# Down-projection tail in three token parts instead of two: one step of a hybrid decoder layer on one Trainium2 core

## The chip, the cores and the metric

The kernel runs on one core of a Trainium2 chip. The time is device microseconds from the launch of the one program to its end. The kernel before takes 2843.49 us (median of three runs, 2843.31 to 2844.28). The profiled execution, to which every row below belongs, is a fourth run of 2844.88 us; its instructions span 2842.7 us of that.

Names of engines: PE is TensorE's matmul side, PEld its weight loads, DVE the vector engine, ACT the scalar engine, POOL GpSimd, SP the engine that issues most DMAs. An AP is an access pattern, PSUM the memory that matmuls write.

## The reference

One layer of a decoder. 512 prompt tokens and 8 x 4 sample tokens, 544 columns in all, go through the same weights:

```
h = rmsnorm(x);  proj = h @ w_in          # mixer: SSD heads and a conformer convolution group
x = x + concat(y, u) @ w_out
h = rmsnorm(x);  u = causal_dwconv(h @ w_up)
g, v = split(u);  x = x + (silu(g) * v) @ w_down      # 43*128 inputs -> 2048 outputs
y = rmsnorm(x, norm_final_w)              # xf * rsqrt(mean(xf * xf) + 1e-5) * w
```

The change touches the last part of `@ w_down` and the final norm. The norm's mean goes over all 2048 outputs of a token, so no token can be scaled before every output tile of that token is finished.

## The kernel before, in words

Tokens are columns: an activation tile is 128 channels by 544 tokens, held as `[128, 2, 272]`, two halves of `NH` = 272 columns. A product in full precision is made of three passes in a rounded 4-byte type (`F32R`): every operand is split in a high and a low part, and `mms` issues weight-high times input-high, weight-high times input-low and weight-low times input-high, all into one PSUM tile. Each of these matmuls is preceded by its own load of a 128x128 weight tile, so the program has as many weight loads as matmuls.

The down-projection adds up 43 input tiles `a` (128 channels each) into 16 output tiles `xres`. Chunks of inputs are taken in turn by a list of work items. The last chunk, `ktail` = 39 with `ntail` = 4 input tiles, is held back: its activations are in `Ah` and `Al`, its weights for all 16 output tiles are loaded and split during the items before (`keep_prep`) and stay in SBUF as `keep[t]`. What is left at the very end is `last_half`: 16 output tiles, 4 inputs, 3 passes, 2 token halves.

`last_half` is written out in order, and every engine runs its instructions in that order. It goes over the halves on the outside and the 16 output tiles inside. For one tile and one half it issues

- 12 matmuls of 272 columns into an `aux` PSUM tile (`paux` has four of them),
- on DVE the sum with the residual `x` (L1512),
- on ACT the square of `x` (L1514) and a copy scaled with the norm weight into `ot`, one tile for two output tiles (L1523),
- on POOL the running sum of the squares (L1518; the last square is not added but goes to the next step by itself).

When a half is complete, `rs_half` sums the squares over the partitions with two matmuls by a matrix of ones (L1486), and DVE and ACT work out the reciprocal root (L1490 to L1497). For the first half this is laid behind the tiles t = 1 to 4 of the second, and `scale_out`, which multiplies an `ot` tile by the root (L1457) and stores it (L1458), behind the tiles after them. For the second half there is nothing left to lay it behind: `run_now(rs_half(1))` and eight `scale_out` stand one after another.

Of the kernel before, what the change touches and what calls it, by code (L numbers as in the profile page):

```python
# [10 lines left out]
AF = mybir.ActivationFunctionType  # L11
ALU = mybir.AluOpType
# [3 lines left out]
NH = 272  # L16
# [9 lines left out]
EPS = 1e-5  # L26
# [3 lines left out]
def hymba_step_kernel(ctx: ExitStack, tc: tile.TileContext, a: dict):  # L30
    nc = tc.nc
    V, G, S, T, Y = nc.vector, nc.gpsimd, nc.scalar, nc.tensor, nc.sync
# [24 lines left out]
    def nm(p):  # L57
        cnt[0] += 1
        return f"{p}{cnt[0]}"

    def slot(p, shape=None, dt=F32, side=False):
        return (Cur.side if side else slots).tile(shape or [128, 2, NH], dt, tag="s", name=nm(p))

    def aux(shape=None):
        return paux.tile(shape or [128, 512], F32, tag="a", name=nm("ax"))
# [11 lines left out]
    def flat(t):  # L77
        return t.rearrange("p h x -> p (h x)")

    def halves(ap):  # L80
        return ap.rearrange("p (h x) -> p h x", h=2)
# [106 lines left out]
    def drain_later():  # L188
        while later:
            later.popleft()()  # L190
# [29 lines left out]
    def mms(outs, hfs, h, l, nk, k0, K, rhs):  # L220
        for kk in range(nk):
            k = k0 + kk
            xh, xl = rhs(k)
            c = slice(kk * 128, kk * 128 + 128)
            passes = ((h, xh, k == 0, False), (h, xl, False, l is None and k == K - 1), (l, xh, False, k == K - 1))
            for w, x, first, last in passes[:2 if l is None else 3]:
                for o, hf in zip(outs, hfs):
                    T.matmul(o, lhsT=w[:, c], rhs=x[:, hf, :], start=first, stop=last)  # L228


    ones = const.tile([128, 128], F32, name="ones")
# [23 lines left out]
    def run_now(gen):  # L255
        for _ in gen:
            pass
# [9 lines left out]
    with tc.manual_schedule():  # L267
# [20 lines left out]
        nw = const.tile([128, 5, 16], F32, name="nw")  # L288
        Y.dma_start(out=nw, in_=a["nvec"])
        NW_MIX, NW_SSD, NW_FFN, NW_FIN, DSK = range(5)  # L290
# [800 lines left out]
        xres, xs, T_t = {}, {}, {}  # L1091
# [267 lines left out]
        Ah, Al, ar = {}, {}, {}  # L1359
# [74 lines left out]
        k0 = 0  # L1434
        for c, (n, pn) in enumerate(DOWN):
            q = len(items)
# [10 lines left out]
        ktail, ntail = k0, HID - k0  # L1447
        a_prep(range(ktail, HID), len(items) - 16)

        fin = {}  # L1450

        ot = {}

        def scale_out(i, hf):

            o = ot.pop((i, hf))
            V.tensor_tensor(o, o, fin[hf, "r"].unsqueeze(1).to_broadcast([128, 2, NH]), ALU.mult)  # L1457
            Y.dma_start(out=a["o_y"][i, hf], in_=flat(o))  # L1458

        keep = {}  # L1460

# [17 lines left out]

        keep_prep(ktail, ntail, len(items) - 16)  # L1480

        def rs_half(hf):
            p = aux()
            accs = [fin[hf], fin[hf, "last"]]
            for i, q in enumerate(accs):
                T.matmul(p[:, 0:NH], lhsT=ones, rhs=q[:, 0:NH], start=i == 0, stop=i == 1)  # L1486
            v = slot("fv")
            r, t = v[:, 1, :], slot("ft")[:, 0, :]
            v = v[:, 0, :]
            V.tensor_scalar(v, p[:, 0:NH], 1.0 / 2048.0, EPS, ALU.mult, ALU.add)  # L1490
            S.activation(r, v, AF.Sqrt)
            yield
            V.reciprocal(r, r)  # L1493
            yield
            V.tensor_tensor(t, r, r, ALU.mult)
            V.scalar_tensor_tensor(t, t, -0.5, v, ALU.mult, ALU.mult)
            V.scalar_tensor_tensor(r, t, 1.5, r, ALU.add, ALU.mult)  # L1497
            fin[hf, "r"] = r
            yield

        def last_half(k0, n):
            gen = []
            todo = deque()
            for hf in range(2):
                if hf:
                    gen.append(rs_half(0))
                for t in range(16):
                    h, l = keep[t]
                    ps = aux()
                    mms([ps[:, 0:NH]], (hf,), h, l, n, 0, n, lambda k: (Ah[k0 + k], Al[k0 + k]))  # L1510
                    x = xres[t][:, hf, :]
                    V.tensor_tensor(x, ps[:, 0:NH], x, ALU.add)  # L1512
                    sq = slot("sq", [128, NH])
                    S.activation(sq, x, AF.Square)  # L1514
                    if t == 0:
                        fin[hf] = sq
                    elif t < 15:
                        G.tensor_tensor(fin[hf], fin[hf], sq, ALU.add)  # L1518
                    else:
                        fin[hf, "last"] = sq  # L1520
                    if t % 2 == 0:
                        ot[t // 2, hf] = slot("ot")
                    S.activation(ot[t // 2, hf][:, t % 2, :], x, AF.Copy, scale=nw[:, NW_FIN, t:t + 1])  # L1523
                    if gen and t >= 1:
                        if next(gen[0], 1) == 1:
                            gen.clear()
                            todo.extend(range(8))
                    if todo:
                        scale_out(todo.popleft(), 0)
            while todo:  # L1530
                scale_out(todo.popleft(), 0)
            run_now(rs_half(1))
            for i in range(8):
                scale_out(i, 1)


        run_jobs()
# [10 lines left out]
        for i in range(3):  # L1548
            n = min(29, 86 - 29 * i)
# [20 lines left out]
            product(q)  # L1570
        evac(len(items) - 1)
        drain_later()
        last_half(ktail, ntail)
        for name in list(pools)[::-1]:
            swap(None, name)

# [107 lines left out]
```

## Time and profile before

| what | us |
|---|---|
| median of three runs | 2843.49 |
| the profiled execution | 2844.88 |
| its span, first to last instruction | 2842.7 |
| PE busy in the span | 2795.5 |
| first residual sum of `last_half` (L1512) begins | 2779.84 |
| last residual sum of `last_half` begins | 2827.62 |
| end of the span | 2842.7 |

PE is busy for 98% of the span, so the first question is what keeps it busy and the second what comes after its last matmul. In the views, times are from the start of the span; `x12` counts instructions, `[0.38 <-POOL sq L1518]` is how long the engine had been idle and what ended that. The profiled execution lies 1.4 us over the median of the runs, and 2.2 us of it lie outside the span.

### The profile page before, as it was taken

The page shows a single profiled execution, that of the slowest core. Times are in us where ns is not written, and L with a number is a line of the kernel's source. Part 1 is how long each engine was busy: PE and PEld are TensorE (multiplying, and loading weights), DVE is VectorE, ACT ScalarE, POOL GpSimd, SP SyncE. Part 2 cuts the span into 40 slices and gives each one's busy share as a digit, 9 for nine tenths or more (in the row PEclk, how much of TensorE's full clock was granted, in tenths as well). Part 3 has the DMA queues.
Part 4 walks back from the last instruction along what each step waited for, and adds up shares of the span by engine and source line. Part 5 has one row for each costly group of instructions (what it writes and reads, how often), then busy time and mean ns, then how long its engine had stood idle before and what let it go on. Part 6 is the DMA issues. An engine that isn't in the chain of part 4 may idle for free. (4 is left out here: it accounts for less than half of the span.)

```text
span 2842.7 us, 55478 instructions
## 1 busy us (share of the span) xinstructions
PE 2795.5 (98%) x22214; PEld 2755.1 (97%) x22214; DVE 2090.9 (74%) x3180; ACT 1210.9 (43%) x1792; POOL 905.5 (32%) x922
## 2 busy tenths in 40 slices
PE   7999999999999999999999999999999999999998
PEld 7999998999999999999999999999999999999997
DVE  7576565777777778335488888888888887778775
ACT  4545444333333324333344444444444443344344
POOL 4466666766676765511100000000000000100103
PEclk9999999999999999999999999999999999999999
DMA  4233342433333343444567776777777776765761
GB/s 164 82 112 114 97 137 88 131 104 103 106 101 91 98 157 111 134 140 134 148 158 187 192 194 185 193 188 189 194 191 185 196 191 208 172 182 158 178 185 64
DMA packets 194371, 422.29 MB, mean 149 GB/s; under 512 B 38080, under 2 KB 42816, under 8 KB 194112
## 3 DMA queue, kind: packets, MB, share of 16 engines
q1 hardware_dynamic: 177120, 361.07, 40.9%
q0 software_dynamic: 16992, 57.68, 11.5%
q8 instruction: 174, 2.85, 0.4%
q14 instruction: 85, 0.70, 0.1%
HBM read 376.25 MB, written 42.41 MB: 147 GB/s over the span
## 5 line engine op out<-in xcount | busy, mean ns | idle before, releaser
L1276 PE MATMUL st<-Th,sl 128*128 128x272 f32 x2640 | 762.4, 289 | 1.8 <-DVE sl L1258 1.8
L1274 PE MATMUL st<-Th,sh 128*128 128x272 f32 x2640 | 762.3, 289 | 1.5 <-ACT sh L1249 1.5
L1275 PE MATMUL st<-Tl,sh 128*128 128x272 f32 x2640 | 761.9, 289 | 0.0
L118 POOL TENSOR_TENSOR wl<-raw,wh 128x512 fp32r<-128x512 f32 x336 | 450.0, 1342 | 421.5 <-ACT wh L117 358.6
L1249 ACT CAST sh<-wr 128x1024 fp32r<-128x1024 f32 (+3 forms) x343 | 327.1, 954 | 417.1 <-PE st L1275 338.9
L1276 PEld LDWEIGHTS st<-Th,sl 128*128 128x128 f32 x2640 | 496.8, 188 | 2.7 <-DVE sl L1258 2.7
L1274 PEld LDWEIGHTS st<-Th,sh 128*128 128x128 f32 x2640 | 496.8, 188 | 1.7 <-ACT sh L1249 1.7
L1275 PEld LDWEIGHTS st<-Tl,sh 128*128 128x128 f32 x2640 | 496.8, 188 | 0.0
L228 PE MATMUL mm<-xh,wh 128*128 128x272 f32 x2304 | 487.1, 293 | 7.3 <-ACT xh L312 7.3
L228 PE MATMUL mm<-xl,wh 128*128 128x272 f32 x2304 | 479.2, 289 | 5.1 <-DVE xl L314 5.1
L117 ACT CAST wh<-raw 128x512 fp32r<-128x512 f32 x416 | 255.5, 616 | 528.4 <-PE mm L228 418.2
L228 PE MATMUL mm<-xh,wl 128*128 128x272 f32 x2304 | 478.0, 288 | 0.0
L1258 DVE TENSOR_TENSOR sl<-wr,sh 128x1024 fp32r<-128x1024 f32 (+3 forms) x343 | 378.1, 1102 | 55.2 <-ACT sh L1249 55.1
L228 PEld LDWEIGHTS mm<-xh,wh 128*128 128x128 f32 x2304 | 365.3, 188 | 20.2 <-issue 10.4
L228 PEld LDWEIGHTS mm<-xl,wh 128*128 128x128 f32 x2304 | 365.3, 188 | 6.5 <-DVE xl L314 6.5
L228 PEld LDWEIGHTS mm<-xh,wl 128*128 128x128 f32 x2304 | 364.9, 188 | 0.0
L1226 POOL DMA_DIRECT2D wr<-in_w_up x86 | 75.1, 873 | 834.3 <-DVE ws L1240 266.7
L937 DVE SCALAR_TENSOR_TENSOR ax<-w,cfw,ax 128x512 f32<-128x512 f32 x448 | 302.2, 747 | 5.8 <-ACT ax L913 5.8
L1249 ACT CAST sh<-ws 128x1024 fp32r<-128x1024 f32 (+1 forms) x118 | 117.1, 992 | 259.2 <-DVE ws L1236 144.6
L1258 DVE TENSOR_TENSOR sl<-ws,sh 128x1024 fp32r<-128x1024 f32 (+1 forms) x118 | 136.1, 1153 | 31.3 <-ACT sh L1249 21.9
L1226 POOL DMA_DIRECT2D wr<-in_w_down x32 | 27.9, 873 | 366.6 <-DVE pd L1400 145.9
L118 DVE TENSOR_TENSOR wl<-raw,wh 128x512 fp32r<-128x512 f32 x80 | 70.2, 883 | 95.4 <-ACT wh L117 95.4
(316 smaller groups left out, 4985.7 us busy)
## 6 DMA issues: line engine op xcount, KB each, us to landing
wr<-in_w_up SPq DMA_DIRECT2D x215, 512.0 KB, 4.9
raw<-in_w_in SPq DMA_DIRECT2D x292, 256.0 KB, 3.1
wr<-in_w_up POOLq DMA_DIRECT2D x86, 512.0 KB, 7.9
wr<-in_w_down SPq DMA_DIRECT2D x96, 384.0 KB, 3.4
raw<-in_w_out SPq DMA_DIRECT2D x128, 256.0 KB, 3.0
wr<-in_w_down POOLq DMA_DIRECT2D x32, 384.0 KB, 5.6
ad<-ra SPq DMA_DIRECT2D x43, 272.0 KB, 9.1
ar<-ad SPq DMA_DIRECT2D x43, 272.0 KB, 4.1
```

The costliest lines, as they stand in the source:

```text
L117: S.copy(h[:, :n], r[:, :n])
L118: (cur["wl"] or eng).tensor_tensor(l[:, :n], r[:, :n], h[:, :n].bitcast(F32), ALU.subtract)
L228: T.matmul(o, lhsT=w[:, c], rhs=x[:, hf, :], start=first, stop=last)
L937: V.scalar_tensor_tensor(p, w[:, i:i + 512], wt(i), p, ALU.mult, ALU.add)
L1226: G.dma_start(out=t, in_=more, accum_op=ALU.add)
L1249: S.copy(h, src)
L1258: V.tensor_tensor(l, src, h.bitcast(F32), ALU.subtract)
L1274: T.matmul(outs[0], lhsT=h[:, c], rhs=xh_, start=k == 0, stop=False)
L1275: T.matmul(outs[0], lhsT=h[:, c], rhs=xl_, start=False, stop=False)
L1276: T.matmul(outs[0], lhsT=l[:, c], rhs=xh_, start=False, stop=k == o.K - 1)
```

## The change

The last four input tiles are no longer worked through in two halves of 272 columns but in three parts: the first half whole, then the second half in two pieces of 136 columns. `PARTS` lists them as half, first column, width. `rs_half` becomes `rs_part`, `last_half` becomes `last_parts`; root, scaling and store of each part are laid behind the tiles t = 1 and later of the part after it, and only those of the last part stand at the end. All tiles of a part have the part's width; the store of a part writes its piece of each row of the output.

```diff
+        PARTS = [(0, 0, NH), (1, 0, NH // 2), (1, NH // 2, NH // 2)]
+
+        def scale_out(i, part):
+
+            hf, c0, n = PARTS[part]
+            o = ot.pop((i, part))
+            V.tensor_tensor(o, o, fin[part, "r"].unsqueeze(1).to_broadcast([128, 2, n]), ALU.mult)
+            Y.dma_start(out=halves(a["o_y"][i, hf])[:, :, c0:c0 + n], in_=o)
...
-        def rs_half(hf):
+        def rs_part(part):
+            n = PARTS[part][2]
             p = aux()
-            accs = [fin[hf], fin[hf, "last"]]
+            accs = [fin[part], fin[part, "last"]]
             for i, q in enumerate(accs):
-                T.matmul(p[:, 0:NH], lhsT=ones, rhs=q[:, 0:NH], start=i == 0, stop=i == 1)
+                T.matmul(p[:, 0:n], lhsT=ones, rhs=q[:, 0:n], start=i == 0, stop=i == 1)
...
-        def last_half(k0, n):
-            gen = []
+        def last_parts(k0, K):
             todo = deque()
-            for hf in range(2):
-                if hf:
-                    gen.append(rs_half(0))
+            for part, (hf, c0, n) in enumerate(PARTS):
+                gen = [rs_part(part - 1)] if part else []
                 for t in range(16):
                     h, l = keep[t]
                     ps = aux()
-                    mms([ps[:, 0:NH]], (hf,), h, l, n, 0, n, lambda k: (Ah[k0 + k], Al[k0 + k]))
-                    x = xres[t][:, hf, :]
-                    V.tensor_tensor(x, ps[:, 0:NH], x, ALU.add)
+                    mms([ps[:, 0:n]], (hf,), h, l, K, 0, K, lambda k: (Ah[k0 + k][:, :, c0:c0 + n], Al[k0 + k][:, :, c0:c0 + n]))
+                    x = xres[t][:, hf, c0:c0 + n]
+                    V.tensor_tensor(x, ps[:, 0:n], x, ALU.add)
...
                     if gen and t >= 1:
                         if next(gen[0], 1) == 1:
                             gen.clear()
-                            todo.extend(range(8))
+                            todo.extend((i, part - 1) for i in range(8))
                     if todo:
-                        scale_out(todo.popleft(), 0)
-            while todo:
-                scale_out(todo.popleft(), 0)
-            run_now(rs_half(1))
+                        scale_out(*todo.popleft())
+                while todo:
+                    scale_out(*todo.popleft())
+            run_now(rs_part(part))
             for i in range(8):
-                scale_out(i, 1)
+                scale_out(i, part)
```

On PE, where the program before ends, these are its last matmuls: the end of output tile 15 in the second half, and the two that sum the squares (`Ah`, `Al` are activations, `kh`, `kl` kept weights, `ax` the PSUM tile, `sq` the squares).

```order
L228 MATMUL ax_33873<-Ah_32781,kh_33243 128x272
L228 MATMUL ax_33873<-Al_32782,kh_33243 128x272
L228 MATMUL ax_33873<-Ah_32781,kl_33244 128x272
L1486 MATMUL ax_33890<-sq_33583,ones 128x272
L1486 MATMUL ax_33890<-sq_33887,ones 128x272
```

At the same place of the changed program the tile's matmuls have 136 columns, and the first tile of the third part follows with the weights of tile 0 once more:

```order
L228 MATMUL ax_33873<-Ah_32781,kh_33243 128x136
L228 MATMUL ax_33873<-Al_32782,kh_33243 128x136
L228 MATMUL ax_33873<-Ah_32781,kl_33244 128x136
L228 MATMUL ax_33890<-Ah_32645,kh_32651 128x136
L228 MATMUL ax_33890<-Al_32646,kh_32651 128x136
L228 MATMUL ax_33890<-Ah_32645,kl_32652 128x136
```

The 192 matmuls of 272 columns of the second half have become 384 of 136, each with its weight load, and the sum of squares of the second part stands 24 matmuls further on, behind two tiles of the third.

On DVE this is the end of the program before, from the last residual sum to the first scalings of `ot` (`fv` holds the root):

```order
L1512 TENSOR_TENSOR xres_28693<-ax_33873,xres_28693 128x272
L1490 TENSOR_SCALAR fv_33893<-ax_33890 128x272
L1493 RECIPROCAL fv_33893<-fv_33893 128x272
L1495 TENSOR_TENSOR ft_33894<-fv_33893 128x272
L1496 SCALAR_TENSOR_TENSOR ft_33894<-ft_33894,fv_33893 128x272
L1497 SCALAR_TENSOR_TENSOR fv_33893<-ft_33894,fv_33893 128x272
L1457 TENSOR_TENSOR ot_33585<-ot_33585,fv_33893 128x544
L1457 TENSOR_TENSOR ot_33629<-ot_33629,fv_33893 128x544
```

And this is the end of the changed one:

```order
L1515 TENSOR_TENSOR xres_28693<-ax_34194,xres_28693 128x136
L1495 TENSOR_SCALAR fv_34214<-ax_34211 128x136
L1498 RECIPROCAL fv_34214<-fv_34214 128x136
L1500 TENSOR_TENSOR ft_34215<-fv_34214 128x136
L1501 SCALAR_TENSOR_TENSOR ft_34215<-ft_34215,fv_34214 128x136
L1502 SCALAR_TENSOR_TENSOR fv_34214<-ft_34215,fv_34214 128x136
L1461 TENSOR_TENSOR ot_33906<-ot_33906,fv_34214 128x272
L1461 TENSOR_TENSOR ot_33950<-ot_33950,fv_34214 128x272
```

The steps are the same and stand in the same order, each with half the columns; in both programs eight scalings stand at the end, and SP stores behind each.

## Rows read from the trace of the kernel before

**Rows 1.** The page, busy time and share of each engine.

```profile
PE 2795.5 (98%) x22214; PEld 2755.1 (97%) x22214; DVE 2090.9 (74%) x3180; ACT 1210.9 (43%) x1792; POOL 905.5 (32%) x922
```

**Rows 2.** Chain that ended last, from 2780 us: start, us, what.

```profile
2779.93 25.46 PE ax L228 x203
2805.39 0.92 PE ax L1486 x4
2806.30 19.77 PE ax L228 x156
...
2827.96 1.35 PE ax L1486 x4
...
2830.28 1.86 DVE fv L1493
```

**Rows 3.** Timeline of DVE from 2775 us: start, us, engine, line, operation.

```profile
2802.40 0.44 DVE L1512 TENSOR_TENSOR xres<-ax,xres 128x272 f32<-128x272 f32 x1 [1.06 <-PE ax L228]
...
2820.38 0.71 DVE L1457 TENSOR_TENSOR ot<-ot,fv 128x544 f32<-128x544 f32 x1
...
2827.62 0.44 DVE L1512 TENSOR_TENSOR xres<-ax,xres 128x272 f32<-128x272 f32 x1 [1.08 <-PE ax L228]
...
2833.66 5.17 DVE L1457 TENSOR_TENSOR ot<-ot,fv 128x544 f32<-128x544 f32 x8
```

**Rows 4.** Groups by form, PE and PEld: line, operation, shapes, count | busy us, mean ns.

```profile
L228 PE MATMUL ax<-Ah,kh 128*128 128x272 f32 x128 | 37.1, 290 | 0.0
...
L228 PEld LDWEIGHTS ax<-Ah,kh 128*128 128x128 f32 x128 | 24.1, 188 | 0.0
...
L655 PEld LDWEIGHTS ax<-MT,xdt 128*64 128x64 f32 x256 | 14.8, 136 | 4.3 <-ACT wh L117 2.1
```

**Rows 5.** Timeline of PEld about 66 us, the weight loads of ten short matmuls.

```profile
66.31 0.96 PEld L387 LDWEIGHTS ax<-cst,dtT 64*128 64x128 f32 x8
67.20 0.30 PEld L388 LDWEIGHTS ax<-cst,dtS 64*128 64x128 f32 x2
```

**Rows 6.** Timeline of PE in the same stretch, the first eight of these matmuls.

```profile
66.31 1.07 PE L387 MATMUL ax<-cst,dtT 64*128 64x32 f32 x8
```

**Rows 7.** Timeline of PEld at 177 us, two loads of the rounded type.

```profile
176.96 0.30 PEld L228 LDWEIGHTS mm<-xh,wh 128*128 128x128 f32 x2
```

**Rows 8.** Timeline of PEld at 1431 us.

```profile
1431.60 0.28 PEld L1274 LDWEIGHTS st<-Th,sh 128*128 128x128 f32 x1
1431.77 0.33 PEld L1275 LDWEIGHTS st<-Tl,sh 128*128 128x128 f32 x1
```

**Rows 9.** Stretches: us, busy us (count) of PE, PEld, DVE, ACT, POOL, granted clock, DMA.

```profile
1425.00:1431.00 6.00, 4.00 (x28) 3.33 (x26) 4.14 (x6) 2.51 (x3) 0.00 (x0) 1.00 0.10 24
1431.70:1435.00 3.30, 3.30 (x16) 3.30 (x16) 2.59 (x6) 1.68 (x3) 0.00 (x0) 0.50 0.46 146
2806.00:2828.00 22.00, 21.62 (x171) 21.36 (x169) 15.81 (x27) 13.40 (x30) 11.52 (x14) 1.00 0.27 102
```

**Rows 10.** Groups by form, DVE, reciprocals of two widths.

```profile
L1493 DVE RECIPROCAL fv<-fv 128x272 f32<-128x272 f32 x2 | 3.7, 1854 | 0.8 <-ACT fv L1491 0.8
...
L402 DVE RECIPROCAL sm<-sm 128x160 f32<-128x160 f32 x1 | 1.2, 1153 | 0.0
```

**Rows 11.** Groups by form, ACT, one operation at two widths.

```profile
L1249 ACT CAST sh<-wr 128x640 fp32r<-128x640 f32 x16 | 11.6, 727 | 13.2 <-PE st L228 5.2 <-issue 4.6 <-ACT Ah L1118 1.9
...
L1118 ACT CAST Ta<-ar 128x272 fp32r<-128x272 f32 x12 | 5.0, 413 | 0.0
```

**Rows 12.** Timeline of SP, the last stores.

```profile
2834.45 4.79 SPq L1458 DMA_DIRECT2D out_o_y<-ot  x8
```

**Rows 13.** DMA from 2834 us to 2842.7 us: queue, packets, MB, share of 16 engines.

```profile
q1 hardware_dynamic: 1152, 2.23, 66.4%
```

**Rows 14.** DMA from 369.9 to 372.9 us, a store of short rows.

```profile
DMA packets 60, 0.01 MB, mean 5 GB/s; under 512 B 58, under 2 KB 58, under 8 KB 60
...
q1 hardware_dynamic: 60, 0.01, 2.3%
```

More of the change, by code (lines that the diff above doesn't have):

```diff
@@ L1452, in hymba_step_kernel @@
         ot = {}
[L1454 to L1458, printed above, removed]
+        PARTS = [(0, 0, NH), (1, 0, NH // 2), (1, NH // 2, NH // 2)]
[4 more added lines that the diff above has]
+            Y.dma_start(out=halves(a["o_y"][i, hf])[:, :, c0:c0 + n], in_=o)
         keep = {}
@@ L1480, in hymba_step_kernel @@
         keep_prep(ktail, ntail, len(items) - 16)
-        def rs_half(hf):
+        def rs_part(part):
+            n = PARTS[part][2]
             p = aux()
-            accs = [fin[hf], fin[hf, "last"]]
+            accs = [fin[part], fin[part, "last"]]
             for i, q in enumerate(accs):
-                T.matmul(p[:, 0:NH], lhsT=ones, rhs=q[:, 0:NH], start=i == 0, stop=i == 1)
+                T.matmul(p[:, 0:n], lhsT=ones, rhs=q[:, 0:n], start=i == 0, stop=i == 1)
             v = slot("fv")
-            r, t = v[:, 1, :], slot("ft")[:, 0, :]
-            v = v[:, 0, :]
-            V.tensor_scalar(v, p[:, 0:NH], 1.0 / 2048.0, EPS, ALU.mult, ALU.add)
+            r, t = v[:, 1, 0:n], slot("ft")[:, 0, 0:n]
+            v = v[:, 0, 0:n]
+            V.tensor_scalar(v, p[:, 0:n], 1.0 / 2048.0, EPS, ALU.mult, ALU.add)
             S.activation(r, v, AF.Sqrt)
@@ L1497, in rs_half @@
             V.scalar_tensor_tensor(r, t, 1.5, r, ALU.add, ALU.mult)
-            fin[hf, "r"] = r
+            fin[part, "r"] = r
             yield
-        def last_half(k0, n):
-            gen = []
+        def last_parts(k0, K):
             todo = deque()
-            for hf in range(2):
-                if hf:
-                    gen.append(rs_half(0))
+            for part, (hf, c0, n) in enumerate(PARTS):
+                gen = [rs_part(part - 1)] if part else []
                 for t in range(16):
@@ L1509, in last_half @@
                     ps = aux()
-                    mms([ps[:, 0:NH]], (hf,), h, l, n, 0, n, lambda k: (Ah[k0 + k], Al[k0 + k]))
-                    x = xres[t][:, hf, :]
-                    V.tensor_tensor(x, ps[:, 0:NH], x, ALU.add)
-                    sq = slot("sq", [128, NH])
+                    mms([ps[:, 0:n]], (hf,), h, l, K, 0, K, lambda k: (Ah[k0 + k][:, :, c0:c0 + n], Al[k0 + k][:, :, c0:c0 + n]))
+                    x = xres[t][:, hf, c0:c0 + n]
+                    V.tensor_tensor(x, ps[:, 0:n], x, ALU.add)
+                    sq = slot("sq", [128, NH])[:, 0:n]
                     S.activation(sq, x, AF.Square)
                     if t == 0:
-                        fin[hf] = sq
+                        fin[part] = sq
                     elif t < 15:
-                        G.tensor_tensor(fin[hf], fin[hf], sq, ALU.add)
+                        G.tensor_tensor(fin[part], fin[part], sq, ALU.add)
                     else:
-                        fin[hf, "last"] = sq
+                        fin[part, "last"] = sq
                     if t % 2 == 0:
-                        ot[t // 2, hf] = slot("ot")
-                    S.activation(ot[t // 2, hf][:, t % 2, :], x, AF.Copy, scale=nw[:, NW_FIN, t:t + 1])
+                        ot[t // 2, part] = slot("ot", [128, 2, n])
+                    S.activation(ot[t // 2, part][:, t % 2, :], x, AF.Copy, scale=nw[:, NW_FIN, t:t + 1])
                     if gen and t >= 1:
@@ L1572, in hymba_step_kernel @@
         drain_later()
-        last_half(ktail, ntail)
+        last_parts(ktail, ntail)
         for name in list(pools)[::-1]:
```

## The prediction, on record before the changed kernel was timed

> **What bounds the kernel now.** I read the busy times first: PE 98%, its weight loads 97%, DVE 74% [rows 1]. The chain of waits comes next, over the last 63 us: in the tail of the down-projection it lies on PE's matmuls without a break until the last one, and from there on it runs through the norm and the scalings on DVE [rows 2]. So a change here has two accounts: what PE's stream of matmuls costs, and what stands behind its last matmul.
>
> PE's stream: 203 matmuls in 25.46 us are 0.1254 us from one to the next [rows 2]. A group's mean duration of 290 ns [rows 4] is not that: matmuls overlap in the pipeline, and only the distance between starts is paid. Every matmul has a weight load of its own, and the loads too stand at 97%: two activities share PE, and one may be the limit as soon as the other shrinks.
>
> Behind the stream: the last residual sum starts at 2827.62 [rows 3] and the span ends at 2842.70, so the exposed tail is 15.08 us. It holds the rest of the sums of squares, the reciprocal of 1.86 [rows 2], the eight scalings of 5.17 [rows 3] and the stores.
>
> **Matmuls.** The second half's 192 matmuls of 272 columns (16 tiles, 4 inputs, 3 passes) go: 192 x 0.1254 = 24.08 us. 384 of 136 columns come. Their price is the whole question, and the profile of before has none of this width in this type. From below: if only columns cost, half of 0.1254, 0.063. From above: as much as now, 0.1254. In between lies what a weight load costs when the matmul is too short to hide it. Ten matmuls of only 32 columns, each with a load of 128 weight columns, show it: from the first load at 66.31 to the ninth at 67.20 are 8 steps of 0.111 us [rows 5], though 32 columns need far less; the matmuls follow at the loads' pace [rows 6]. These are in the unrounded type. For the rounded one, after a change of shape, where the first matmul cannot begin before its load is done, two loads end 0.30 us after the first began, one takes 0.19 [rows 4], so the second began 0.11 after the first [rows 7]. And a load of 64 columns lasts 136 ns against 188 for 128 [rows 4]: 0.81 ns per column, 0.104 us for 128. Three readings, one answer: a load holds its path for about 0.11 us and the next waits for it. Today that hides under 0.1254; under 0.063 it cannot. I take the row that is a steady stream, 0.111: 384 x 0.111 = 42.6 us, so +18.5 us.
>
> The Trainium skill speaks of such pairs too (TensorE: Matmul & The Clock Gate, section Back-to-back issue gap): a stream of load and matmul is said to sustain about 81 ns per matmul at 128 columns and 131 at 512. By it the 384 would cost about 31 us, and the edit +7.0. The trace does not bear it out at the one width they share a scale for: 272 columns take 0.1254 here, nearly what the Trainium skill gives for 512.
>
> **Sums over partitions.** The two matmuls by ones show as four of 0.23 us each, 0.92 in all [rows 2]. Before, four lay inside the stream; now eight do, four of full and four of half width: +0.46 us on PE.
>
> **Behind the last matmul.** The order of steps is the same, each at half width. DVE: 0.71 us at 544 columns and 0.44 at 272 [rows 3], 1.0 ns per column, so 0.14 less for each of the residual sum and four small steps of the root, and 0.27 less for the first scaling: -0.95. ACT: 727 ns at 640 and 413 at 272 columns [rows 11], 0.85 ns per column: square and root -0.23. The reciprocal: 1854 at 272 and 1153 at 160 [rows 10], 6.3 ns per column: -0.85. The two matmuls behind the last square: -0.23. Together -2.26.
>
> Then eight stores. Now they keep the DMA engines busy for 66.4% of 8.7 us, 5.78 us, for 5.17 us of scalings [rows 3, 12, 13]: the transfers set the end, not DVE. Half the bytes, but rows of 544 bytes instead of 2176, so 2048 packets. The 1152 packets (1936 bytes in the mean) took 16 x 5.78 / 1152 = 0.080 us each [rows 13]; 60 short ones of some 200 bytes 16 x 3.0 x 0.023 / 60 = 0.018 [rows 14]. On a line between them 544 bytes cost 0.030, the train 2048 x 0.030 / 16 = 3.9 us: -1.9. If bytes alone counted it would be 2.9 (-2.9); if a short packet cost as much as a long one, 10.2 (+4.5). DVE needs 8 x 0.44 = 3.5 and stays beneath. Tail: -4.2, between -5.2 and +2.2.
>
> **What I cost at nothing.** The first part is unchanged. Root, scalings and stores of the second part go behind the third. In the old second half, 22.0 us with just that work for the first half, DVE was busy 15.8, ACT 13.4, POOL 11.5 [rows 9]; a part now has half the columns in its own steps, and at 0.111 lasts 21.3 us plus the sums. What covers it is PE's stream, 1.33 us per tile. Without it PE would wait once DVE lags by more than three tiles (four PSUM tiles), and the second part is the place, where the first part's full-width root and scalings queue ahead of residual sums on DVE. The sum of squares of part two makes PE wait only if POOL is over two tiles (2.7 us) late. The new stores on SP are queued ahead of nothing but other stores.
>
> **The sum.** +18.5 + 0.46 - 4.2 = +14.8 us. On the profiled execution, 2844.88 (span 2842.7 and 2.2 around it), that is 2859.7; it lay 1.4 over the median of the runs, so against 2843.49 I forecast 2858.3.
>
> **Rivals.**
> 1. Only columns cost. PE's stream stays at 24.1, and the change is +0.46 - 4.2 = -3.7: 2839.8, not slower. For it: loads and matmuls already overlap in the stream. Against it: rows 5 and 7. It decides as long as a short matmul stays under 0.063 + 3.7 / 384 = 0.072 us.
> 2. Loads are partly hidden, as if the next could begin before the one ahead has been taken up. Midway, 0.087: 33.4 us, +9.3 - 3.7 = +5.6, 2849.1. Against it: 22214 loads for 22214 matmuls [rows 1], and the eight even steps of 0.111. The Trainium skill's figure for 128 columns (TensorE: Matmul & The Clock Gate, Back-to-back issue gap) would give +7.0 - 3.7, 2846.8.
> 3. Nothing is gained by half width: 0.1254 stays. 48.15 us, +24.1 - 3.7 = +20.3: 2863.8. For it: 272 columns may already be paced by the load and some 15 ns more, since the rounded type has no short matmul in this trace.
> 4. The clock or a serial load. After PE has had pauses (4.00 busy of 6.00) the granted clock is found at 0.50, 1.2 GHz [rows 9], and there a load is 0.17 apart from the next [rows 8]; if the array, streaming half the time, were granted that, or if a load waited for the matmul ahead to end (0.111 + 0.063), the stream would cost 384 x 0.17 = 65.3: +41.2 - 3.7 = +37.5, 2881. Against it: PE never stops issuing, and today a load starts with the matmul ahead of it.
> 5. The change does not move what it says: the last part's chain could still wait for work of the part before on DVE. It has twelve tiles, 16 us, for eight scalings; I give it nothing of its own.
>
> **How the numbers follow.** Forecast 62%, rival 1 7%, rival 2 9%, rival 3 13%, rival 4 9%. The range from 2847 to 2866 takes in the forecast with the dear end of the stores (+6.4), rival 3 and most of rival 2; it leaves out rivals 1 and 4 and the quick end of 2, under 2 in 10. 0.2%, about 5.7 us, is what a measurement can tell from no change here: rival 1 and half of rival 2 lie within it, a quicker tail with rival 1 barely beyond. Faster 2%, same 12%, slower 86%.
>
> **What will show it.** Weight loads and matmuls of 136 columns 0.111 apart, 1.33 us from residual sum to residual sum in parts two and three, 1.5 in part one; PE's chain from part one's end longer by 19 us; from the last residual sum to the end of the span 10.9 instead of 15.1 us; no PE wait for DVE in part two; granted clock 1.00 throughout. A spacing under 0.072 would make the forecast wrong in sign, one of 0.17 in size; a tail over 15 us would put the error on the stores.

## The result, and the profile after

The changed kernel takes 2861.54 us (median of 4 runs, 2860.33 to 2862.47), the kernel before, run beside it on the same chip, 2843.64 (4 runs, 2843.31 to 2844.28). The ratio is 1.0062, 95% interval 1.0045 to 1.0080: slower, by 17.9 us at the medians. Forecast were 2858.3 (2847 to 2866), +14.8.

The profiled execution of after took 2860.33, the fastest of the four; its span is 2857.9, so 15.2 us longer than that of before. First the page's busy times, to be held against [rows 1]; the line numbers of the tail are now 3 to 5 higher.

```profile
PE 2816.0 (99%) x22410; PEld 2777.2 (97%) x22410; DVE 2096.4 (73%) x3209; ACT 1217.4 (43%) x1825; POOL 906.1 (32%) x936
```

There are 196 more matmuls and 196 more weight loads: 192 in the stream and four for the sum over partitions of one more part. PE grows by 20.5 us, DVE by 5.5; so the place to look is PE's stream. The chain of waits of after (start, us, what) answers to [rows 2]:

```profile
2778.91 24.56 PE ax L228 x199
2803.48 0.96 PE ax L1491 x4
2804.44 21.39 PE ax L228 x192
2825.84 0.51 PE ax L1491 x4
2826.34 18.73 PE ax L228 x168
...
2847.07 1.01 DVE fv L1498
```

192 matmuls of 136 columns in 21.39 us are 0.1114 us each, 168 in 18.73 the same; before, 203 of 272 columns in 25.46 were 0.1254 [rows 2]. Half the columns, 11% less time. The groups by form (line, operation, shapes, count | busy us, mean ns) show how little a mean duration says of this:

```profile
L228 PEld LDWEIGHTS ax<-Ah,kh 128*128 128x128 f32 x192 | 36.6, 191 | 0.0
...
L228 PE MATMUL ax<-Ah,kh 128*128 128x136 f32 x128 | 35.3, 276 | 0.0
...
L228 PE MATMUL ax<-Ah,kh 128*128 128x272 f32 x64 | 18.4, 287 | 0.0
```

One matmul lasts 276 ns at 136 columns and 287 at 272; a load lasts 191 in the mean of all three parts, where it was 188 [rows 4]. What is paid is the distance between starts.

The timeline of DVE (start, us, operation) gives the three points that divide the end of the program, as [rows 3] did: the last residual sum of part one, that of the last part, and the last scalings. The sum before the last shows the pace, 1.34 us.

```profile
2800.88 0.44 DVE L1515 TENSOR_TENSOR xres<-ax,xres 128x272 f32<-128x272 f32 x1 [1.06 <-PE ax L228]
...
2843.75 0.30 DVE L1515 TENSOR_TENSOR xres<-ax,xres 128x136 f32<-128x136 f32 x1 [1.04 <-PE ax L228]
2845.09 0.30 DVE L1515 TENSOR_TENSOR xres<-ax,xres 128x136 f32<-128x136 f32 x1 [1.04 <-PE ax L228]
...
2849.11 2.90 DVE L1461 TENSOR_TENSOR ot<-ot,fv 128x272 f32<-128x272 f32 x8
```

| stretch | before | after | difference |
|---|---|---|---|
| span's start to last sum of part one | 2802.40 | 2800.88 | -1.52 |
| from there to the last residual sum | 25.22 | 44.21 | +18.99 |
| last residual sum to first scaling of the last part | 6.04 | 4.02 | -2.02 |
| first scaling to the span's end | 9.04 | 8.79 | -0.25 |
| span | 2842.7 | 2857.9 | +15.2 |

The first line is none of the change: the program is the same there, and the offset is in the trace long before the tail. The short loads that stood at 66.31 [rows 5] are found in after (timeline of PEld) at

```profile
64.50 0.96 PEld L387 LDWEIGHTS ax<-cst,dtT 64*128 64x128 f32 x8
```

In the profiles of the experiments below the same row starts between 64.82 and 66.33. At the end of part one, up to which all of these programs but E5's are the same, they lie further apart: between 2800.88 (after) and 2804.97 (E6). E2 is at 64.88 in the one place and at 2804.86 in the other, so the scatter is not the start's alone. A term is therefore to be read between two points of the tail, not from the spans.

The stretches (us, busy us and count of PE, PEld, DVE, ACT, POOL; granted clock, DMA share, GB/s) show the middle line of the table with nothing in it but PE at work, at the full clock of 2.4 GHz:

```profile
2800.90:2845.10 44.20, 44.18 (x393) 43.88 (x391) 23.25 (x59) 21.87 (x67) 13.98 (x29) 1.00 0.21 77
```

Behind the stream, SP's timeline (start, us from the first issue's start to the last one's end) and the summary of that line (durations of one in ns, min/median/max) answer to [rows 12], the DMA view from 2849.9 to the end to [rows 13]. The two lines after it are SP's waits for DVE behind the last residual sum, before and after (us in total, times, longest):

```profile
2849.94 5.30 SPq L1462 DMA_DIRECT2D out_o_y<-ot  x8
```

```profile
L1462 SPq DMA_DIRECT2D out_o_y<-ot x24: 332/534/670, 2810.8 to 2854.7; - x24
```

```profile
q1 hardware_dynamic: 2176, 1.11, 45.6%
```

```profile
SPq L1458 <- DVE ot L1457: 13.1, 8, 11.4
```

```profile
SPq L1462 <- DVE ot L1461: 8.6, 1, 8.6
```

DVE does its eight scalings in 2.90 us, but SP needs 5.30 for its eight issues, 0.66 from one to the next: a store of part one, 128 rows of 2176 bytes, takes SP 0.332, one of the new parts, 256 rows of 544, 0.534 and more. SP waits for DVE only once, ahead of the first store. The DMA engines are busy 45.6% of the 8.0 us from 2849.9 to the end, 3.65 us: less than SP, so they wait for it. Before, SP waited for DVE ahead of each of the eight stores, so its 4.79 us [rows 12] were the pace of the scalings and not of its issues, and the transfers, 5.78 us, took longest.

### The profile page after: what moved, and what is told of

It reads as the page before. It is cut to its first block, busy times and chain, and to the rows that moved or that the text cites. A ratio compares the mean times of both kernels' runs of the same rounds, so it can differ in the third digit from the quotient of the medians.

```text
span 2857.9 us, 55998 instructions
## 1 busy us (share of the span) xinstructions
PE 2816.0 (99%) x22410; PEld 2777.2 (97%) x22410; DVE 2096.4 (73%) x3209; ACT 1217.4 (43%) x1825; POOL 906.1 (32%) x936
```

## The experiments

Theory: a weight load of 128 columns holds its path for about 0.111 us, a matmul short enough is paced by it, and the 18.5 us of the stream are this alone. For the tail: the issues on SP pace the last stores, not the transfers. The rivals are in the expectations. E3 starts from the kernel before, the others from the changed one.

**E3. Narrow matmuls alone.** The second half's matmuls are split into twice 136 columns, into the same PSUM tile; norm, scalings and stores stay at 272.

```
-  mms([ps[:, 0:NH]], (hf,), h, l, n, 0, n, lambda k: (Ah[k0 + k], Al[k0 + k]))
+  for c0, w in ((0, NH),) if hf == 0 else ((0, NH // 2), (NH // 2, NH // 2)):
+      mms([ps[:, c0:c0 + w]], (hf,), h, l, n, 0, n,
+          lambda k: (Ah[k0 + k][:, :, c0:c0 + w], Al[k0 + k][:, :, c0:c0 + w]))
```

> The kernel before with one edit: in the second half each output tile's 12 matmuls of 272 columns become 24 of 136; norm, scaling and stores keep the half's width of 272. Theory L (a load of 128 weight columns holds its path for 0.111 us and sets the pace of a narrow matmul): 384 x 0.1114 instead of 192 x 0.1254, +18.7 us, tail unchanged at 15.1 us, so 2862.3 against 2843.6 (ratio 1.0066). Rival D (half or more of the stream's excess comes from what was laid behind it, DVE or ACT in the way of PSUM tiles): under +10 us here, since nothing is laid behind a third part.

Measured: 2862.80 (2861.65 to 2866.10, 5 runs) against 2844.59 for before on that chip (2843.33 to 2846.30, 9 runs); ratio 1.0065, 1.0052 to 1.0077. Chain of waits, and timeline of DVE:

```profile
2806.41 0.97 PE ax L1486 x4
2807.37 37.49 PE ax L228 x336
```

```profile
2801.13 0.44 DVE L1513 TENSOR_TENSOR xres<-ax,xres 128x272 f32<-128x272 f32 x1 [1.06 <-PE ax L228]
...
2842.20 0.44 DVE L1513 TENSOR_TENSOR xres<-ax,xres 128x272 f32<-128x272 f32 x1 [2.24 <-PE ax L228]
2844.88 0.44 DVE L1513 TENSOR_TENSOR xres<-ax,xres 128x272 f32<-128x272 f32 x1 [2.24 <-PE ax L228]
...
2850.91 5.17 DVE L1457 TENSOR_TENSOR ot<-ot,fv 128x544 f32<-128x544 f32 x8
```

336 matmuls in 37.49 us: 0.1116. A tile, now of 24 matmuls, takes 2.68. From the last sum of the first half to that of the second are 43.75 us, 18.5 more than before, and the tail, to the span's end at 2860.1, is 15.2, as before. So the stream's cost comes with the narrow matmuls alone, twice as many with a load each. None of these 18.5 us is due to the new order of norm and scalings, and a wait for DVE as their cause is refuted; the 18.99 of after have one more sum over partitions in them.

**E6. Weight loads of 64 columns.** In parts two and three the matmuls take only the first 64 of the 128 weight columns, with the same 136 moving columns, the same count and the same order; the upper 64 outputs of each tile lack the last four inputs.

```
-      c = slice(kk * 128, kk * 128 + 128)
+      c = slice(kk * 128, kk * 128 + m)
...
-  mms([ps[:, 0:n]], ...)
+  mms([ps[0:m, 0:n]], ..., m)          # m = 64 in parts two and three
```

> The changed kernel with one edit: in parts two and three each matmul uses only the first 64 of the 128 weight columns, so the lower 64 outputs of each tile are made as before and the last four inputs are left out of the other 64. Columns of the moving operand stay at 136. Theory L: a load of 64 columns takes 0.052 to 0.055 us, so the matmul's own columns set the pace, 0.063 to 0.072 apart, and the 384 take 24 to 28 us instead of 42.8: some 15 to 18 us less than the changed kernel, 2843 to 2846. Rival C (a fixed price of about 0.1 us per matmul whatever its weights): still 0.111, 2861.

Measured: one run, 2849.77. Its groups by form, and DVE's timeline at both ends of the stretch:

```profile
L228 PE MATMUL ax<-Ah,kh 128*64 128x136 f32 x128 | 26.2, 235 | 1.0 <-DVE xres L1516 0.9
...
L228 PEld LDWEIGHTS ax<-Ah,kh 128*64 128x64 f32 x128 | 17.4, 136 | 1.9 <-DVE xres L1516 1.5
```

```profile
2804.97 0.44 DVE L1516 TENSOR_TENSOR xres<-ax,xres 128x272 f32<-128x272 f32 x1 [1.06 <-PE ax L228]
2805.73 0.29 DVE L1516 TENSOR_TENSOR xres<-ax,xres 64x136 f32<-64x136 f32 x1 [0.32 <-PE ax L228]
2806.49 0.29 DVE L1516 TENSOR_TENSOR xres<-ax,xres 64x136 f32<-64x136 f32 x1 [0.47 <-PE ax L228]
...
2834.45 0.29 DVE L1516 TENSOR_TENSOR xres<-ax,xres 64x136 f32<-64x136 f32 x1 [0.51 <-PE ax L228]
2835.25 0.29 DVE L1516 TENSOR_TENSOR xres<-ax,xres 64x136 f32<-64x136 f32 x1 [0.51 <-PE ax L228]
```

Where nothing holds PE up, at both ends of the stretch, twelve matmuls now take 0.76 to 0.80 us instead of 1.34: 0.063 to 0.067 each. The moving columns are what they were, so the 0.111 is neither a price of 136 columns nor a fixed price of any matmul; it is gone when the load is halved. The edit halves with the load also the rows that a matmul writes, and no run here parts the two. What remains is so near to 0.063, half of 0.1254, that this run cannot say whether columns or the shorter load now set the pace. From 2804.97 to 2835.25 are 30.28 us instead of 44.21, less gain than expected, because a faster PE uses up the cover: it now waits for residual sums on DVE, as the releaser in both groups shows, and is busy 28.16 of 30.40 us in the stretches. The tail, to the span's end at 2848.0, is as in after (12.8). This run's first part ended 4.1 us later than that of after, so its total says less than its stretch.

**E1. The stores of a part in whole rows.** Each store of parts two and three writes 128 rows of 1088 bytes instead of 256 of 544; the outputs' order is changed to fit.

```
-  Y.dma_start(out=halves(a["o_y"][i, hf])[:, :, c0:c0 + n], in_=o)
+  Y.dma_start(out=a["o_y"][i, hf][:, 2 * c0:2 * c0 + 2 * n], in_=flat(o))
```

> The changed kernel with another layout of the output in memory: each part's 2 x 136 columns of a row lie side by side, so a store of parts two and three has 128 rows of 1088 bytes instead of 256 of 544. Theory I (SP's issue of a store of 256 rows, 0.53 to 0.56 us and 0.66 from one to the next, sets the pace of the last eight): issue back to 0.33, the train then goes at DVE's 0.36 to 0.40, 2.1 to 2.4 us less than the changed kernel; tail 10.5 instead of 12.8, 2859.3. Rival P (what is slow is the writing of short rows): also less, by about half, since the rows are twice as long: 1 us.

Measured: 2859.80 (2858.29 to 2860.09, 5 runs), ratio to before 1.0051, 1.0038 to 1.0065; that interval overlaps the one of after, so the gain over after is not shown by the times. In the profile it is: the timelines of DVE and of SP read

```profile
2847.27 0.30 DVE L1515 TENSOR_TENSOR xres<-ax,xres 128x136 f32<-128x136 f32 x1 [1.04 <-PE ax L228]
...
2851.29 2.90 DVE L1461 TENSOR_TENSOR ot<-ot,fv 128x272 f32<-128x272 f32 x8
```

```profile
2852.12 3.78 SPq L1462 DMA_DIRECT2D out_o_y<-ot  x8
```

and the line's summary of one issue

```profile
L1462 SPq DMA_DIRECT2D out_o_y<-ot x24: 332/332/395, 2813.0 to 2855.5; - x24
```

The eight issues take 3.78 us instead of 5.30, and from the last residual sum to the end of the span (2858.3) are 11.0 us instead of 12.8. The same bytes in half the rows: SP pays by rows, 0.33 for 128, whether of 1088 or of 2176 bytes, and 0.53 for 256. The gain, 1.8 us, is less than the 2.1 to 2.4 expected: the stores did not come down to DVE's pace of 0.36, but follow each other by nearly 0.5. Here rows, packets and the time of an issue all shrink together, so this alone doesn't tell issue from transfer.

**E2. The same stores, issued from two queues.** Every other store of the last part is issued by ACT, which is idle then; rows and packets are those of after.

```
-  Y.dma_start(...)
+  (S if part == 2 and i % 2 else Y).dma_start(...)
```

> The changed kernel with one edit: of the last part's eight stores every second one is issued from ACT's queue, the rows of 544 bytes stay. Theory I: two issuers at 0.56 each make 0.33 per store, the train goes at DVE's 0.36 to 0.45, 1.6 to 2.2 us less than the changed kernel, 2859.6. Rival P: no change, tail 12.8.

Measured: 2860.67 (2858.55 to 2862.81, 5 runs), ratio 1.0055, 1.0043 to 1.0068; again not to be told from after by its time. Its timelines of DVE, SP and ACT, and the DMA view from 2853 to the end (queue, packets, MB, share):

```profile
2849.07 0.30 DVE L1515 TENSOR_TENSOR xres<-ax,xres 128x136 f32<-128x136 f32 x1 [1.04 <-PE ax L228]
```

```profile
2853.91 2.53 SPq L1462 DMA_DIRECT2D out_o_y<-ot  x4
```

```profile
2853.91 2.99 ACTq L1462 DMA_DIRECT2D out_o_y<-ot  x4
```

```profile
q10 hardware_dynamic: 1088, 0.56, 24.5%
q1 hardware_dynamic: 1088, 0.56, 24.1%
```

The issues are over in 2.99 us instead of 5.30, and the tail (to 2860.6) is 11.5 instead of 12.8. 2.3 us of issue became 1.3 of tail, less than the 1.6 to 2.2 expected, because now the transfers are the limit. The DMA view from 2856.9, when the last issue is done, to the end (40 slices, busy tenths) shows engines that are full until about 2859:

```profile
DMA  9999999999999999999971000000000000000000
```

48.6% of 7.6 us are 3.7 us for 2176 packets, so 0.027 us each on one of 16 engines: near the 0.030 by which the prediction priced a packet. That price was nearly right; the issue in front of it had been left out.

**E4. Parts of 272, 208 and 64 columns.** The changed kernel with another cut of the second half.

```
-  PARTS = [(0, 0, NH), (1, 0, NH // 2), (1, NH // 2, NH // 2)]
+  PARTS = [(0, 0, NH), (1, 0, 208), (1, 208, 64)]
```

> The changed kernel with one edit: the second half is cut in 208 and 64 columns instead of 136 and 136. Theory L (weight load as floor): both widths go at 0.111, so part two lasts 21.4 us and part three 21.4 us apart from the sums, as with 136 and 136. Rival C (a fixed price plus columns, on the line through 0.1254 at 272 and 0.1115 at 136): 0.119 at 208 and 0.104 at 64, 22.8 and 20.0 us. Same total by both, so the spacing of each part decides. The tail gets shorter by a smaller norm (about 2 us) and its stores have 256 rows of 256 bytes, issued in the same 0.56 us: 10 to 11 us.

Measured: one run, 2873.56, span 2871.4. Chain of waits, then a piece of PE's timeline, then two stretches:

```profile
2804.94 21.36 PE ax L228 x192
2826.30 0.79 PE ax L1491 x4
2827.09 32.66 PE ax L228 x168
```

```profile
2827.18 0.28 PE L228 MATMUL ax<-Ah,kh 128*128 128x64 f32 x1
...
2830.08 0.28 PE L228 MATMUL ax<-Ah,kl 128*128 128x64 f32 x1
...
2831.17 0.40 PE L228 MATMUL ax<-Ah,kl 128*128 128x64 f32 x1
2831.39 0.40 PE L228 MATMUL ax<-Ah,kh 128*128 128x64 f32 x1
```

```profile
2826.00:2830.00 4.00, 4.00 (x36) 4.00 (x35) 2.22 (x5) 1.37 (x5) 0.64 (x2) 1.00 0.02 4
2831.00:2859.00 28.00, 28.00 (x133) 28.00 (x133) 6.72 (x20) 5.45 (x22) 3.55 (x12) 0.50 0.18 61
```

Two results. At full clock, 192 matmuls, 168 of them of 208 columns and the last 24 of 64, cost 0.1113 each (21.36 / 192); those of 64 columns by themselves cost 0.1115 (26 steps from 2827.18 to 2830.08). With 136 these are three widths at one price, which is the load's; a fixed price plus columns, 0.119 and 0.104, is refuted. The other result was not expected: from about 2830.3 on the granted clock is 0.50, 1.2 GHz, though PE had not paused. Matmuls then stand 0.213 apart (2.56 us from one residual sum to the next, twelve matmuls), and the last 168 take 32.66 us instead of 18.73. That is the clock of rival 4 of the prediction, not at 136 columns but at 64; it was seen in this one run. The tail, from 2859.77 to the span's end, is 11.6 us, where 10 to 11 were expected.

**E5. Two parts of 288 and 256 columns.** The cut lies across the halves, each part's rows are contiguous, and with two parts the order of norm and scalings is that of before.

```
-  PARTS = [(0, 0, NH), (1, 0, NH // 2), (1, NH // 2, NH // 2)]
+  PARTS = [(0, 288), (288, 256)]
...
-  mms([ps[:, 0:n]], (hf,), h, l, K, 0, K,
-      lambda k: (Ah[k0 + k][:, :, c0:c0 + n], Al[k0 + k][:, :, c0:c0 + n]))
+  mms([ps[:, 0:n]], (0,), h, l, K, 0, K, lambda k: (cols(Ah[k0 + k], c0, n), cols(Al[k0 + k], c0, n)))
```

> Two parts again, but cut across the two halves: 288 columns first, 256 last, each part's rows side by side in memory. Theory L: columns set the pace at both widths (0.133 and 0.118, 0.461 ns per column, above the floor of 0.111), so the stream's 384 matmuls take 48.2 us as in the kernel before, and the tail is shorter by 16 columns: about 0.3 us in the norm's steps and 0.3 in the stores. 2843.0 against 2843.6, no change that a measurement can tell. Rival C (every matmul below 272 pays more than its columns): 0.1237 at 256 and 0.127 at 288, the same 48.1 us in all, but other spacings.

Measured: 2843.32 (2842.41 to 2847.67, 11 runs) against 2844.82 (2843.15 to 2849.01, 15 runs); ratio 0.9997, 0.9988 to 1.0006: no difference. DVE's timeline, two sums of each part and the last:

```profile
2800.18 0.46 DVE L1517 TENSOR_TENSOR xres<-ax,xres 128x288 f32<-128x288 f32 x1 [1.12 <-PE ax L228]
2801.76 0.46 DVE L1517 TENSOR_TENSOR xres<-ax,xres 128x288 f32<-128x288 f32 x1 [1.12 <-PE ax L228]
...
2822.66 0.42 DVE L1517 TENSOR_TENSOR xres<-ax,xres 128x256 f32<-128x256 f32 x1 [0.76 <-PE ax L228]
2824.09 0.42 DVE L1517 TENSOR_TENSOR xres<-ax,xres 128x256 f32<-128x256 f32 x1 [1.00 <-PE ax L228]
2825.50 0.42 DVE L1517 TENSOR_TENSOR xres<-ax,xres 128x256 f32<-128x256 f32 x1 [0.99 <-PE ax L228]
```

1.58 us for 12 matmuls of 288 columns is 0.1317, 1.41 to 1.43 for 256 is 0.118 to 0.119. Over 16 tiles of each that is 48.0 us, where twice 24.08 for 272 is 48.2: in this range the time goes with the columns, at 0.46 ns each. The tail, to the span's end at 2840.3, is 14.8 instead of 15.1, too little to measure. By this rate 0.111 is reached at some 240 columns; that crossing is worked out, no run lies on it.

## Why the prediction was right, and where it was off

**The stream of matmuls: right.** +18.5 and +0.46 were forecast, +18.99 came. The step that carried it was to take the price of a short matmul from other instructions, the ten short ones in a steady stream [rows 5] and the pair behind a pause [rows 7], and not from the 290 ns of a group or from half of 0.1254. Of the reason given for that pair, that the first matmul cannot begin before its load is done, the trace shows nothing: PE's timeline has the matmul from 176.96 on too, like its load. What it shows is that the two loads begin 0.11 apart. E3 shows that the narrow matmuls alone do it, E6 that halving the load takes it away, E4 that 64 and 208 columns pay the same.

**Rivals 1 to 3: refuted.** A spacing of 0.1114 is above 0.072 and 0.087 and below 0.1254. The Trainium skill's 81 ns per matmul at 128 columns (TensorE: Matmul & The Clock Gate, Back-to-back issue gap) does not hold for this stream at 136. The section LDWEIGHTS (loading the stationary operand) of the same page of the Trainium skill gives a load columns / 1.2 in ns, by estimate 107 for 128. That agrees with the spacings of 111 here, not with the 188 to 191 that the profile gives as the duration of one load.

**Rival 4: refuted for this change, but the mechanism is real.** The granted clock stayed at 1.00 through 44.2 us of 136 columns. At 64 columns it fell to half in E4, in the one run of it, and a matmul then cost 0.213, not the 0.17 that [rows 8] suggested. The argument "PE never stops issuing" was no reason against it, as E4 shows; that 136 columns were spared is a measurement, and why is not settled here.

**Rival 5: refuted.** Between the last residual sum and the last part's scalings stand only that part's own steps, 4.02 us.

**The norm behind the last sum: right.** Forecast -1.99 up to the first scaling (-2.26 less the 0.27 of the scaling itself), measured -2.02. The profile of E1 has the same 4.02 us there.

**The store train: the step that failed.** "The transfers set the end, not DVE" was carried over from before, and the train priced at 3.9 us, -1.9; with the first scaling's 0.27 that is -2.2 where -0.25 came. The transfers do take about that (3.65 in after, 3.7 in E2). But the issue on SP was priced nowhere: it went from 0.332 to 0.534 us with twice the rows, and eight of them, with what lies between, are 5.30 us, longer than transfers and scalings. E1 takes rows away and E2 halves SP's share at the same rows and packets; both shorten the train, E1 by 1.8 us and E2 by 1.3, each in one profile. The tail as a whole, -2.27 for -4.2, lay within its bounds of -5.2 and +2.2.

**Cover: right.** In part two DVE fell behind and some residual sums waited for DVE instead of PE, but PE was busy 44.18 of 44.20 us. E6 shows the size of that cover: with matmuls of 0.063 to 0.067 PE does wait for DVE.

**The time.** Stream and tail measure +18.99 - 2.27 = +16.7; the medians differ by 17.9. Of the 3.2 us between forecast and median 1.9 are the tail. The rest, 1.3, is no larger than the scatter of part one's end between the profiles, 4.1 us, and nothing here gives it a cause. In the two profiles the part ahead of the change goes the other way, -1.52, so that the +15.2 of their spans lies near +14.8 by luck.

## What to carry to other kernels

Before cutting matmuls narrower, find the distance between weight loads that nothing else paces; if the cut brings the matmul beneath it, the work is paid by count, as here, and not by columns. When a store is cut, price three things apart, its producer, its issue and its transfer, and count rows for the second and packets for the third: the longest of them may be another than before. Read terms of a small change between marks near it: here the same stretch of program ahead of the change ended up to 4.1 us apart in two profiles.

## What the runs showed of the hardware that was not expected

- A matmul of this type with 128 weight columns costs 0.111 us at 64, 136 and 208 columns alike (E4, after), and 0.118 to 0.119, 0.1254 and 0.1317 at 256, 272 and 288 (E5, before).
- SP's issue of a store grew with its rows, 0.332 us for 128 and 0.534 for 256; on ACT the 256 rows took 0.56 to 0.73 (E2).
- The granted clock fell to 0.50, 1.2 GHz, in a stream of 64-column matmuls in which PE was busy 4.00 of 4.00 us (E4, one run), and a matmul then cost 0.213.
